# A fixed order for the end of the down projection: the last three row pieces transposed and squared in parts, their sums and scalings interleaved

## The chip, the cores and the metric

The kernel runs on one core of a Trainium2 chip. The metric is the device time of one execution in microseconds, the median of the runs.

## What is computed

One inference step of a one-layer decoder: a prompt of 1024 positions and 32 sample positions (1056 columns in all) pass through a mixer (windowed attention and retention) and a convolutional FFN. The change lies at the very end of the FFN, in its down projection and the norm behind it:

```python
h = jax.nn.gelu(a, approximate=True) * b
f = h @ w_down                           # 3072 -> 1024
x = x + rms_norm(f, g_post_ffn)          # rms_norm: f * rsqrt(mean(f*f) + EPS) * g
```

All of it is fp32. A product is made of three matmuls of operands split into a high and a low part (`mm3`).

## The kernel before

**Down projection.** `acc0` to `acc7` hold f transposed: each has 128 of the 1024 channels on its partitions and the 1056 positions along the free dimension. The product is computed by a Strassen-like scheme of seven products (`PORD`); S4 is the last. Within S4, `products(p, c, pt, js, ms)` does the k tiles of one third `pt` for one column half `j` and one channel tile (`c`, `e`), summed in a PSUM bank over `pt` 0 to 2. The last two tiles that come out complete are acc2 and then acc3, of the second half of the positions. acc3's last 264 columns are computed in two column pieces (`LASTP`): 136 and then 128 columns, each with 36 matmuls, and each added to acc3 by VectorE.

**Norm.** Rows (positions) are normalized in eleven pieces, `rws`. Pieces 0 to 4 come after S1; pieces 5, 6 and 7 (128, 128 and 16 rows) inside S4; pieces 8 (8 rows), 9 (128) and 10 (128) at the end: 8 and 9 lie in the 136 columns, 10 in the 128. `final` does one piece: eight transposes on TensorE turn columns of acc4 to acc7 (half 1) and of acc0 to acc3 (half 0) into two PSUM banks; ScalarE squares each bank into the tile `y` and sums the squares along the row; VectorE adds the two sums and makes the mean; GpSimd takes the power −1/2 (`rs`); VectorE multiplies each bank by `rs` and the gain into `y` (scaling); then x2 is added in halves (residual) and each half of `y` is written to HBM from SP's queue.

**Buffers.** `y` has three buffers (`tag="c_out", bufs=3`), so that piece 8 takes that of piece 5, 9 that of 6, 10 that of 7: the square of a piece overwrites what the write of the piece three back still reads. PSUM has eight banks in two rings of four: tag `m` for half 1 of the pieces, tag `t` for half 0; the products of the second position half use `t`.

```python
    def ps_8(j=0):
        return psum(p8, "mt"[j])
    for a, n, r in LASTP:
        for pt in range(3):
            products(S4, 1, pt, (1,), (1,), ws[pt], a, n)
        c12 = C(3, 0, 1, 1)[:, a:a + n]
        V.tensor_tensor(out=c12, in0=banks[1, 1, 1], in1=c12, op=add)
        norm(len(r), end=True)
```

**Order.** Each engine runs its instructions in a fixed order that a list scheduler makes at build time from a simulated timeline; `pin(ins)` keeps an instruction where the code has it in relation to other pinned ones of its engine. On the chip each engine waits at the first instruction whose inputs aren't there, and what is queued behind it on that engine waits too.

## Time and profile before

| | us |
|---|---|
| median of 3 runs | 1681.14 |
| the runs | 1680.82, 1681.14, 1684.15 |
| the profiled execution, its own time | 1684.12 |
| its span, from the first to the last instruction | 1682.3 |
| TensorE busy in the span | 1661.6 (99%) |

Busy time is a share of the span; a matmul's end is modelled, so a busy TensorE is not one at its peak. All durations below come from the one profiled execution, which took 2.98 us longer than the median, with 1.8 us of its time outside its span.

### The profile page before, as it was taken

The numbers are of one execution on the slowest core, as the hardware profiler recorded it, in microseconds if no ns is written. First come the engines' busy times: TensorE is split into PE (matmuls) and PEld (weight loads), VectorE is DVE, ScalarE is ACT, GpSimd is POOL, SyncE is SP. The second block draws the span as 40 slices with busy tenths as digits, with TensorE's granted clock in tenths as the row PEclk, the third lists the DMA queues.
The fourth block names the chain that finished last, engine by engine and source line by source line (L and its number), as shares of the span: only waits on it lengthen the run. The fifth ranks groups of instructions, "written<-read, shape, count | busy, mean of one in ns | idle before, by whom it ended". The sixth has DMA issues, their size and how long they took to land.

```text
span 1682.3 us, 31548 instructions
## 1 busy us (share of the span) xinstructions
PE 1661.6 (99%) x12257; PEld 1629.7 (97%) x12257; DVE 1181.2 (70%) x2305; ACT 794.4 (47%) x1727; POOL 341.1 (20%) x551
## 2 busy tenths in 40 slices
PE   8999999999999999999999999999999999999997
PEld 7999999999999999999888999999999999999997
DVE  7768554428586865658857888888888887455476
ACT  6576643223333332455433655555555556443343
POOL 4110110001212122320012412222221233111111
PEclk9999999999999999999999999999999999999999
DMA  7222234534242435377722145444444457866664
GB/s 198 64 74 80 74 97 123 180 106 145 96 152 95 151 102 173 109 247 239 234 94 87 45 156 161 148 155 149 146 146 146 149 162 246 257 183 199 192 184 149
DMA packets 253671, 247.87 MB, mean 147 GB/s; under 512 B 20192, under 2 KB 221568, under 8 KB 253505
## 3 DMA queue, kind: packets, MB, share of 16 engines
q1 hardware_dynamic: 224593, 145.10, 29.6%
q0 software_dynamic: 28928, 100.76, 17.4%
q8 instruction: 96, 1.57, 0.4%
q14 instruction: 54, 0.44, 0.1%
HBM read 171.27 MB, written 74.51 MB: 146 GB/s over the span
## 4 chain that ended last, share of the span: by engine, by line
PE 94%; DMA 2%; issue 2%; DVE 1%; POOL 0%; ACT 0%; SPq 0%; POOLq 0%; DVEq 0%; ACTq 0%
PE ps_mm L259 11%; PE ps_mm L261 11%; PE ps_mm L260 11%; PE ps_m L261 10%; PE ps_m L259 10%; PE ps_m L260 9%; PE ps_t L260 8%; PE ps_t L259 8%; PE ps_t L261 8%; PE ps_a L550 1%; PE ps_c L579 1%; DMA t<-z_d 1%; DMA a_in<-a_d 0%; PE ps_a L796 0%; PE ps_t L332 0%
## 5 line engine op out<-in xcount | busy, mean ns | idle before, releaser
L259 PE MATMUL ps_mm<-xh,w_hi 128*128 128x384 f32 (+1 forms) x888 | 291.8, 329 | 0.5 <-ACT w_hi L247 0.5
L261 PE MATMUL ps_mm<-xh,w_lo 128*128 128x384 f32 (+1 forms) x888 | 290.9, 328 | 0.0
L260 PE MATMUL ps_mm<-xl,w_hi 128*128 128x384 f32 (+1 forms) x888 | 289.5, 326 | 0.1
L227 DVE SCALAR_TENSOR_TENSOR w_lo<-w_raw,w_hi 128x1024 fp32r<-128x1024 f32 x115 | 140.5, 1222 | 115.6 <-ACT w_hi L232 62.8
L259 PEld LDWEIGHTS ps_mm<-xh,w_hi 128*128 128x128 f32 x888 | 168.1, 189 | 1.5 <-ACT w_hi L247 0.8
L260 PEld LDWEIGHTS ps_mm<-xl,w_hi 128*128 128x128 f32 x888 | 168.0, 189 | 1.2 <-issue 0.7
L261 PEld LDWEIGHTS ps_mm<-xh,w_lo 128*128 128x128 f32 x888 | 167.8, 189 | 0.6 <-issue 0.4
L259 PE MATMUL ps_t<-xh,w_hi 128*128 128x264 f32 (+2 forms) x524 | 148.9, 284 | 0.0
L260 PE MATMUL ps_t<-xl,w_hi 128*128 128x264 f32 (+2 forms) x524 | 148.7, 284 | 0.0
L261 PE MATMUL ps_t<-xh,w_lo 128*128 128x264 f32 (+2 forms) x524 | 148.0, 283 | 0.0
L261 PE MATMUL ps_m<-xh,w_lo 128*128 128x264 f32 x512 | 145.5, 285 | 1.3 <-DVE w_lo L227 1.3
L259 PE MATMUL ps_m<-xh,w_hi 128*128 128x264 f32 x512 | 145.7, 285 | 0.0
L260 PE MATMUL ps_m<-xl,w_hi 128*128 128x264 f32 x512 | 145.5, 284 | 0.0
L1233 DVE SCALAR_TENSOR_TENSOR c_out<-u_ext,fconst,c_out 128x1024 f32<-128x1024 f32 x96 | 121.9, 1279 | 2.2
L232 ACT CAST w_hi<-w_raw 128x1024 fp32r<-128x1024 f32 x62 | 65.2, 1052 | 105.6 <-PE ps_t L260 75.4
L261 PEld LDWEIGHTS ps_t<-xh,w_lo 128*128 128x128 f32 x524 | 98.7, 188 | 0.0
L260 PEld LDWEIGHTS ps_t<-xl,w_hi 128*128 128x128 f32 x524 | 98.6, 188 | 0.0
L259 PEld LDWEIGHTS ps_t<-xh,w_hi 128*128 128x128 f32 x524 | 98.6, 188 | 0.0
L261 PEld LDWEIGHTS ps_m<-xh,w_lo 128*128 128x128 f32 x512 | 96.3, 188 | 1.8 <-DVE w_lo L227 1.7
L259 PEld LDWEIGHTS ps_m<-xh,w_hi 128*128 128x128 f32 x512 | 96.2, 188 | 0.1
L260 PEld LDWEIGHTS ps_m<-xl,w_hi 128*128 128x128 f32 x512 | 96.2, 188 | 0.0
L286 POOL TENSOR_TENSOR rs<-ms,mhalf 128x1 f32<-128x1 f32 (+2 forms) x74 | 49.6, 671 | 226.4 <-DVE ms L284 225.9
(429 smaller groups left out, 5135.8 us busy)
## 6 DMA issues: line engine op xcount, KB each, us to landing
w_raw<-in_w_up SPq DMA_DIRECT2D x48, 512.0 KB, 4.7
w_raw<-in_w_in SPq DMA_DIRECT2D x42, 512.0 KB, 4.0
w_raw<-s_d SPq DMA_DIRECT2D x60, 256.0 KB, 3.5
t_d<-t POOLq DMA_DIRECT2D x24, 528.0 KB, 3.9
t<-t_d POOLq DMA_DIRECT2D x24, 528.0 KB, 5.0
t<-in_w_down SPq DMA_DIRECT2D x40, 256.0 KB, 4.7
s_d<-t POOLq DMA_DIRECT2D x20, 512.0 KB, 3.5
w_raw<-in_w_down SPq DMA_DIRECT2D x36, 256.0 KB, 5.0
```

The costliest lines, as they stand in the source:

```text
L227: pinned(V.scalar_tensor_tensor(out=out, in0=in0, scalar=1.0, in1=in1, op0=mult, op1=op))
L232: pinned(S.copy(out=hi, in_=src))
L259: TE.matmul(ps, wh, xh, start=start, stop=False, **kw)
L260: TE.matmul(ps, wh, xl, start=False, stop=False, **kw)
L261: TE.matmul(ps, wl, xh, start=False, stop=stop, **kw)
L286: G.tensor_tensor(out=rs[:r, :c], in0=ms[:r, :c], in1=mhalf[:r, :c], op=ALU.pow)
L550: TE.matmul(ps[:, jj, :], q, kS[s][v][:, kc], start=s == 0, stop=s == 1)
L579: TE.matmul(po[:, v], w, pr[:, s, 2 * v:2 * v + 2, :], start=i == 0 and s == 0, stop=i == len(ops) - 1 and s == 1)
L1233: V.scalar_tensor_tensor(out=c[:, NS:], in0=u[:, g, NU + t:NU + t + SEQ], scalar=sc[t], in1=c[:, NS:], op0=mult, op1=add)
```

## The change

`final` becomes a function that does the early part of a piece and returns three others: `rest` (the remaining sum and the power), `scale` and `residual`. For pieces 8, 9 and 10 the early part transposes and squares half 1 and, as a new and smaller square of 384 columns, what of half 0 is in acc0 to acc2; the last 128 columns, those of acc3, are transposed and squared in `rest`. The mean square is now built up in `ms` with one VectorE instruction a sum: `tensor_scalar` for the first, `scalar_tensor_tensor` for each further one (before: one addition, then one `tensor_scalar`). The early parts of all three pieces stand ahead of acc3's products. The products of the 136 columns get a bank of tag `m`, those of the 128 one of tag `t`, and the matmuls of the second, the late transposes, the sums, scalings and residuals are pinned. The order of the three pieces' scalings and residuals is written out by hand.

```diff
-    def mm3(ps, wh, wl, xh, xl, start, stop, **kw):
...
+    def mm3(ps, wh, wl, xh, xl, start, stop, order=None, **kw):
+        for w, x, a, b in ((wh, xh, start, False), (wh, xl, False, False), (wl, xh, False, stop)):
+            ins = TE.matmul(ps, w, x, start=a, stop=b, **kw)
+            if order is not None:
+                order(ins)
...
+    def transposes(ps, r0, n, ks, hf, last=False):
+        for k in ks:
+            ins = TE.transpose(ps[:n, k * P:(k + 1) * P], acc[4 * hf + k][:, r0:r0 + n], ident)
+            if last:
+                pin(ins)
+
+    def square(y, ps, n, hf, a, b, ss):
+        S.activation(y[:, 512 * hf + a:512 * hf + b], ps[:n, a:b], AF.Square, accum_out=ss)
...
+        def sums(i, hf, a, b):
+            if a == 0:
+                pss[hf] = ps_8(1 - hf)
+            transposes(pss[hf], r0, n, range(a, b), hf, a > 0)
+            square(y, pss[hf], n, hf, P * a, P * b, s2[:, i:i + 1])
+            if i == 0:
+                V.tensor_scalar(out=ms, in0=s2[:, 0:1], scalar1=1.0 / D, scalar2=EPS, op0=mult, op1=add)
+            else:
+                ins = V.scalar_tensor_tensor(out=ms, in0=s2[:, i:i + 1], scalar=1.0 / D, in1=ms,
+                                             op0=mult, op1=add)
+                if i == 2:
+                    pin(ins)
+
+        sums(0, 1, 0, 4)
+        sums(1, 0, 0, 3 if end else 4)
+
+        def rest():
+            if end:
+                sums(2, 0, 3, 4)
+            ins = G.tensor_tensor(out=r, in0=ms, in1=mhalf[:n, :1], op=ALU.pow)
+            if end:
+                pin(ins)
...
-    for a, n, r in LASTP:
-        for pt in range(3):
-            products(S4, 1, pt, (1,), (1,), ws[pt], a, n)
+    def last(i, pts):
+        a, n = LASTP[i][:2]
+        for pt in pts:
+            products(S4, 1, pt, (1,), (1,), ws[pt], a, n, i, pin if i else None)
+
+    def last_done(i):
+        a, n = LASTP[i][:2]
         c12 = C(3, 0, 1, 1)[:, a:a + n]
-        V.tensor_tensor(out=c12, in0=banks[1, 1, 1], in1=c12, op=add)
-        norm(len(r), end=True)
+        pin(V.tensor_tensor(out=c12, in0=banks[1, 1, 1], in1=c12, op=add))
+
+    k = rdone[0]
+    (rest0, sc0, res0), (rest1, sc1, res1), (rest2, sc2, res2) = (final(*rws[i], x2s[i], True)
+                                                                  for i in range(k, k + 3))
+    last(0, range(3))
+    last_done(0)
+    last(1, (0,))
+    rest0()
+    rest1()
+    last(1, (1, 2))
+    sc0(0)
+    res0(0)
+    last_done(1)
+    sc0(1)
+    rest2()
+    for f, x in ((sc1, 0), (res1, 0), (sc1, 1), (res0, 1), (sc2, 0), (res2, 0), (sc2, 1), (res1, 1),
+                 (res2, 1)):
+        f(x)
```

In the order rows below a number behind a tile's name tells buffers of one name apart. `y` and `s2` of piece 7 are 19455 and 19456 in both kernels.

TensorE, before, where acc2's products of 264 columns (into ps_t_19489) end and those of acc3's 136 columns begin:

```order
L261 MATMUL ps_t_19489<-xh_109,w_lo_19525 128x264
L259 MATMUL ps_t_19489<-xh_109,w_hi_19524 128x264
L260 MATMUL ps_t_19489<-xl_110,w_hi_19524 128x264
L261 MATMUL ps_t_19489<-xh_109,w_lo_19525 128x264
L259 MATMUL ps_t_19541<-xh_109,w_hi_19485 128x136
L260 MATMUL ps_t_19541<-xl_110,w_hi_19485 128x136
```

The same place of the changed kernel (its line 260 is the matmul of `mm3`, 1321 the transpose):

```order
L260 MATMUL ps_t_19489<-xl_110,w_hi_19524 128x264
L260 MATMUL ps_t_19489<-xh_109,w_lo_19525 128x264
L1321 MATMUL ps_t_19552<-ident_102,acc0_16787 8x128
L1321 MATMUL ps_t_19552<-ident_102,acc1_16788 8x128
L1321 MATMUL ps_t_19569<-ident_102,acc0_16787 128x128
L1321 MATMUL ps_t_19569<-ident_102,acc1_16788 128x128
L1321 MATMUL ps_m_19579<-ident_102,acc4_16783 128x128
L1321 MATMUL ps_m_19579<-ident_102,acc5_16784 128x128
L1321 MATMUL ps_m_19579<-ident_102,acc6_16785 128x128
L1321 MATMUL ps_m_19579<-ident_102,acc7_16786 128x128
L1321 MATMUL ps_t_19586<-ident_102,acc0_16787 128x128
L1321 MATMUL ps_t_19586<-ident_102,acc1_16788 128x128
```

Ten transposes of pieces 8, 9 and 10 (of acc0, acc1, and of acc4 to acc7 for piece 10) now stand between the two groups of products; before, the early ones of half 0 came after the 136-column products, and piece 10's after all products.

ScalarE, before, from the second square of piece 7 to the end (L1328; y_19579, y_19604 and y_19667 are pieces 8, 9 and 10):

```order
L1328 ACTIVATE y_19455,s2_19456<-ps_t_19463 16x512
L1328 ACTIVATE y_19579,s2_19580<-ps_m_19581 8x512
L1328 ACTIVATE y_19604,s2_19605<-ps_m_19606 128x512
L1328 ACTIVATE y_19579,s2_19580<-ps_t_19587 8x512
L1328 ACTIVATE y_19604,s2_19605<-ps_t_19612 128x512
L1328 ACTIVATE y_19667,s2_19668<-ps_m_19669 128x512
L1328 ACTIVATE y_19667,s2_19668<-ps_t_19675 128x512
```

And in the changed kernel, from the first square of piece 8 to the end (L1326; y_19541, y_19558 and y_19575 are pieces 8, 9 and 10):

```order
L1326 ACTIVATE y_19541,s2_19542<-ps_m_19545 8x512
L1326 ACTIVATE y_19558,s2_19559<-ps_m_19562 128x512
L1326 ACTIVATE y_19575,s2_19576<-ps_m_19579 128x512
L1326 ACTIVATE y_19541,s2_19542<-ps_t_19552 8x384
L1326 ACTIVATE y_19558,s2_19559<-ps_t_19569 128x384
L1326 ACTIVATE y_19575,s2_19576<-ps_t_19586 128x384
L1326 ACTIVATE y_19541,s2_19542<-ps_t_19552 8x128
L1326 ACTIVATE y_19558,s2_19559<-ps_t_19569 128x128
L1326 ACTIVATE y_19575,s2_19576<-ps_t_19586 128x128
```

The first square of piece 10 moved from behind all squares of pieces 8 and 9 to the third place, ahead of every square of half 0 of the three pieces, and half 0's squares are six of 384 and 128 columns in place of three of 512.

VectorE, before, from the last residual of piece 7 through the completion of acc3's last 128 columns (the second row of L1423):

```order
L1337 TENSOR_TENSOR y_19455<-y_19455,x2_19205 16x512
L1423 TENSOR_TENSOR acc3_16790<-ps_t_19541,acc3_16790 128x136
L1331 TENSOR_TENSOR s2_19580<-s2_19580 8x1
L284 TENSOR_SCALAR ms_19594<-s2_19580 8x1
L1331 TENSOR_TENSOR s2_19605<-s2_19605 128x1
L284 TENSOR_SCALAR ms_19619<-s2_19605 128x1
L1335 SCALAR_TENSOR_TENSOR y_19579<-ps_t_19587,rs_19596,g_pf_18227 8x512
L1335 SCALAR_TENSOR_TENSOR y_19579<-ps_m_19581,rs_19596,g_pf_18227 8x512
L1423 TENSOR_TENSOR acc3_16790<-ps_t_19629,acc3_16790 128x128
```

The same stretch of the changed kernel, from just behind piece 7's last residual (L1342 and L1344 make the mean squares, L1466 completes acc3, L1361 scales):

```order
L1342 TENSOR_SCALAR ms_19560<-s2_19559 128x1
L1342 TENSOR_SCALAR ms_19577<-s2_19576 128x1
L1344 SCALAR_TENSOR_TENSOR ms_19543<-s2_19542,ms_19543 8x1
L1344 SCALAR_TENSOR_TENSOR ms_19560<-s2_19559,ms_19560 128x1
L1344 SCALAR_TENSOR_TENSOR ms_19577<-s2_19576,ms_19577 128x1
L1466 TENSOR_TENSOR acc3_16790<-ps_m_19592,acc3_16790 128x136
L1344 SCALAR_TENSOR_TENSOR ms_19543<-s2_19542,ms_19543 8x1
L1344 SCALAR_TENSOR_TENSOR ms_19560<-s2_19559,ms_19560 128x1
L1361 SCALAR_TENSOR_TENSOR y_19541<-ps_t_19552,rs_19544,g_pf_18227 8x512
L1466 TENSOR_TENSOR acc3_16790<-ps_t_19630,acc3_16790 128x128
```

The early sums of all three pieces, piece 10's (ms_19577) last, now stand ahead of the addition that completes acc3's 136 columns; before, that addition stood first.

VectorE, before, from there to its end:

```order
L1335 SCALAR_TENSOR_TENSOR y_19604<-ps_t_19612,rs_19621,g_pf_18227 128x512
L1335 SCALAR_TENSOR_TENSOR y_19604<-ps_m_19606,rs_19621,g_pf_18227 128x512
L1337 TENSOR_TENSOR y_19579<-y_19579,x2_19329 8x512
L1331 TENSOR_TENSOR s2_19668<-s2_19668 128x1
L1337 TENSOR_TENSOR y_19604<-y_19604,x2_19453 128x512
L284 TENSOR_SCALAR ms_19682<-s2_19668 128x1
L1335 SCALAR_TENSOR_TENSOR y_19667<-ps_t_19675,rs_19684,g_pf_18227 128x512
L1335 SCALAR_TENSOR_TENSOR y_19667<-ps_m_19669,rs_19684,g_pf_18227 128x512
L1337 TENSOR_TENSOR y_19667<-y_19667,x2_19480 128x512
```

And in the changed kernel:

```order
L1466 TENSOR_TENSOR acc3_16790<-ps_t_19630,acc3_16790 128x128
L1361 SCALAR_TENSOR_TENSOR y_19541<-ps_m_19545,rs_19544,g_pf_18227 8x512
L1344 SCALAR_TENSOR_TENSOR ms_19577<-s2_19576,ms_19577 128x1
L1361 SCALAR_TENSOR_TENSOR y_19558<-ps_t_19569,rs_19561,g_pf_18227 128x512
L1361 SCALAR_TENSOR_TENSOR y_19558<-ps_m_19562,rs_19561,g_pf_18227 128x512
L1368 TENSOR_TENSOR y_19541<-y_19541,x2_19329 8x512
L1361 SCALAR_TENSOR_TENSOR y_19575<-ps_t_19586,rs_19578,g_pf_18227 128x512
L1361 SCALAR_TENSOR_TENSOR y_19575<-ps_m_19579,rs_19578,g_pf_18227 128x512
L1368 TENSOR_TENSOR y_19558<-y_19558,x2_19453 128x512
L1368 TENSOR_TENSOR y_19575<-y_19575,x2_19480 128x512
```

Before, piece 10's scalings stood behind both residuals of pieces 8 and 9; now only piece 8's residual stands ahead of them, and the residuals of pieces 9 and 10 come last together.

## Rows read from the trace of the kernel before

**Rows 1.** The page: its first line, the busy time of the engines, and the chain that ended last by engine.

```profile
span 1682.3 us, 31548 instructions
...
PE 1661.6 (99%) x12257; PEld 1629.7 (97%) x12257; DVE 1181.2 (70%) x2305; ACT 794.4 (47%) x1727; POOL 341.1 (20%) x551
...
PE 94%; DMA 2%; issue 2%; DVE 1%; POOL 0%; ACT 0%; SPq 0%; POOLq 0%; DVEq 0%; ACTq 0%
```

**Rows 2.** The instructions in order of time on TensorE, where the last products of the program end. Columns: start in us, duration in us, engine, line, operation, tile written and tiles read, shape, count, and the idle time before it with what ended it. L259 to L261 are the three matmuls of `mm3`, L1327 the transposes of `final`.

```profile
1661.97 0.28 PE L261 MATMUL ps_t<-xh,w_lo 128*128 128x264 f32 x1
1662.09 0.23 PE L259 MATMUL ps_t<-xh,w_hi 128*128 128x136 f32 x1
...
1665.95 0.28 PE L261 MATMUL ps_t<-xh,w_lo 128*128 128x136 f32 x1
1666.06 0.82 PE L1327 MATMUL ps_t<-ident,acc 128*8 128x128 f32 x6
1666.64 0.31 PE L259 MATMUL ps_t<-xh,w_hi 128*128 128x128 f32 x1
...
1668.57 0.38 PE L1327 MATMUL ps_t<-ident,acc 128*8 128x128 f32 x2
...
1670.75 0.28 PE L261 MATMUL ps_t<-xh,w_lo 128*128 128x128 f32 x1
1670.86 0.62 PE L1327 MATMUL ps_m<-ident,acc 128*128 128x128 f32 x4
...
1672.28 0.33 PE L1327 MATMUL ps_t<-ident,acc 128*128 128x128 f32 x1 [0.46 <-DVE acc L1423]
```

**Rows 3.** The chain that ended last in order of time, one of its pieces: start in us, us that it holds the chain, engine, tile, line, count.

```profile
1657.03 0.87 PE ps_m L1327 x8
```

**Rows 4.** The instructions in order of time on VectorE at the same place, columns as in the second group. L1335 scales, L1337 adds the residual, L1423 completes acc3, L1331 and L284 make the mean square.

```profile
1662.45 0.73 DVE L1335 SCALAR_TENSOR_TENSOR y<-ps_m,rs,g_pf 16x512 f32<-16x512 f32 x1
...
1671.30 0.73 DVE L1335 SCALAR_TENSOR_TENSOR y<-ps_m,rs,g_pf 8x512 f32<-8x512 f32 x1
1671.96 0.27 DVE L1423 TENSOR_TENSOR acc<-ps_t,acc 128x128 f32<-128x128 f32 x1
1672.15 0.73 DVE L1335 SCALAR_TENSOR_TENSOR y<-ps_t,rs,g_pf 128x512 f32<-128x512 f32 x1
...
1673.47 1.30 DVE L1337 TENSOR_TENSOR y<-y,x 8x512 f32<-8x512 f32 x1
1674.70 0.14 DVE L1331 TENSOR_TENSOR s<-s 128x1 f32<-128x1 f32 x1
1674.77 0.67 DVE L1337 TENSOR_TENSOR y<-y,x 128x512 f32<-128x512 f32 x1
1675.37 0.13 DVE L284 TENSOR_SCALAR ms<-s 128x1 f32<-128x1 f32 x1
1676.23 0.75 DVE L1335 SCALAR_TENSOR_TENSOR y<-ps_t,rs,g_pf 128x512 f32<-128x512 f32 x1 [0.73 <-POOL rs L286]
...
1677.67 1.20 DVE L1337 TENSOR_TENSOR y<-y,x 128x512 f32<-128x512 f32 x1
```

**Rows 5.** The same view of GpSimd (L286 the power −1/2 on one column, L1337 the residual of a first half).

```profile
1672.96 1.26 POOL L1337 TENSOR_TENSOR y<-y,x 128x512 f32<-128x512 f32 x1 [0.25 <-DVE y L1335]
1675.65 0.55 POOL L286 TENSOR_TENSOR rs<-ms,mhalf 128x1 f32<-128x1 f32 x1 [1.42 <-DVE ms L284]
1677.06 1.26 POOL L1337 TENSOR_TENSOR y<-y,x 128x512 f32<-128x512 f32 x1 [0.86 <-DVE y L1335]
```

**Rows 6.** The same view of ScalarE (L232 casts weights, L1328 squares with a sum, whose read-out is an instruction of its own).

```profile
1655.20 1.06 ACT L232 CAST w_hi<-w_raw 128x1024 fp32r<-128x1024 f32 x1 [1.84 <-PE ps_t L260]
...
1656.73 0.59 ACT L1328 ACTIVATE y<-ps_t 128x512 f32<-128x512 f32 x1
...
1657.30 0.57 ACT L1328 ACTIVATE y<-ps_m 16x512 f32<-16x512 f32 x1
...
1664.11 0.60 ACT L1328 ACTIVATE y<-ps_m 128x512 f32<-128x512 f32 x1 [5.00 <-DMA out_y_prompt<-y]
...
1672.65 0.60 ACT L1328 ACTIVATE y<-ps_t 128x512 f32<-128x512 f32 x1 [0.38 <-PE ps_t L1327]
1673.14 0.20 ACT L1328 ACTIVATION_READ_ACCUMULATOR y<-ps_t 128x1 f32 x1
```

**Rows 7.** The writes of y to HBM (L1339, on SP's queue), one stretch of time after another: name and count, duration of the issue in ns (min/median/max), first and last start in us; and the us from issue to landing. First the second write of piece 7, then three writes of pieces 8 and 9, then the last write of the program.

```profile
L1339 SPq DMA_DIRECT2D out_y_prompt<-y x1: 331/331/331, 1664.8 to 1664.8; - x1
...
DMA to landing us min/median/max: 2.5/2.5/2.5
...
L1339 SPq DMA_DIRECT2D out_y_prompt<-y x3: 283/355/382, 1674.8 to 1675.6; - x3
...
DMA to landing us min/median/max: 2.1/2.2/2.3
...
L1339 SPq DMA_DIRECT2D out_y_prompt<-y x1: 332/332/332, 1678.9 to 1678.9; - x1
```

**Rows 8.** ScalarE and then VectorE in order of time some 40 us earlier, where S4's weights are split into w_hi and w_lo.

```profile
1630.12 1.05 ACT L232 CAST w_hi<-w_raw 128x1024 fp32r<-128x1024 f32 x1 [1.28 <-PE ps_m L260]
1633.05 1.06 ACT L232 CAST w_hi<-w_raw 128x1024 fp32r<-128x1024 f32 x1 [1.87 <-PE ps_m L260]
...
1631.41 1.22 DVE L227 SCALAR_TENSOR_TENSOR w_lo<-w_raw,w_hi 128x1024 fp32r<-128x1024 f32 x1
```

More of the change, by code (lines that the diff above doesn't have):

```diff
@@ L256, in wcols @@
         return weights(k, n, [(lambda r: r, src)], **kw)
-    def mm3(ps, wh, wl, xh, xl, start, stop, **kw):
-        TE.matmul(ps, wh, xh, start=start, stop=False, **kw)
-        TE.matmul(ps, wh, xl, start=False, stop=False, **kw)
-        TE.matmul(ps, wl, xh, start=False, stop=stop, **kw)
+    def mm3(ps, wh, wl, xh, xl, start, stop, order=None, **kw):
[3 more added lines that the diff above has]
+                order(ins)
     def sample_cols(t):
@@ L1321, in final @@
         y = fp.tile([P, D], F32, name="y", tag="c_out", bufs=3)[:n]
-        s2 = sml.tile([P, 2], F32, name="s2")[:n]
+        s2 = sml.tile([P, 4], F32, name="s2")[:n]
         pss = {}
-        for hf in (1, 0):
-            ps = ps_8(1 - hf)
-            for k in range(4):
-                TE.transpose(ps[:n, k * P:(k + 1) * P], acc[4 * hf + k][:, r0:r0 + n], ident)
-            S.activation(y[:, 512 * hf:512 * hf + 512], ps[:n], AF.Square,
-                         accum_out=s2[:, hf:hf + 1])
-            pss[hf] = ps
@@ L1331, in final @@
-        V.tensor_tensor(out=s2[:, 0:1], in0=s2[:, 0:1], in1=s2[:, 1:2], op=add)
-        r = rsqrt_mean(s2[:, 0:1], D, n, 1)
-        for hf in range(2):
-            nn = slice(512 * hf, 512 * hf + 512)
-            V.scalar_tensor_tensor(out=y[:, nn], in0=pss[hf][:n], scalar=r, in1=g_pf[:n, nn],
-                                   op0=mult, op1=mult)
-            (G if end and hf == 0 else V).tensor_tensor(out=y[:, nn], in0=y[:, nn], in1=x2[:, nn],
-                                                        op=add)
+        ms, r = (sml.tile([P, 16], F32, name=q)[:n, :1] for q in ("ms", "rs"))
@@ new lines, in final, with scale @@
+        sums(0, 1, 0, 4)
[6 more added lines that the diff above has]
+                pin(ins)
+        def scale(hf):
+            nn = slice(512 * hf, 512 * hf + 512)
+            ins = V.scalar_tensor_tensor(out=y[:, nn], in0=pss[hf][:n], scalar=r, in1=g_pf[:n, nn],
+                                         op0=mult, op1=mult)
+            if end:
+                pin(ins)
@@ L1339, in final, with residual @@
+        def residual(hf):
+            nn = slice(512 * hf, 512 * hf + 512)
+            ins = (G if end and hf == 0 else V).tensor_tensor(out=y[:, nn], in0=y[:, nn], in1=x2[:, nn],
+                                                              op=add)
+            if end:
+                pin(ins)
             ld.dma_start(out=dst[:, nn], in_=y[:, nn])
+        return rest, scale, residual
     rws = ROWS_A22 + ROWS_S4 + [r for d in LASTP for r in d[2]]
@@ L1343, in trunk, with norm @@
     rdone = [0]
-    def norm(n, end=False):
+    def norm(n):
         for _ in range(n):
@@ L1349, in norm @@
             rdone[0] += 1
-            final(*rws[i], x2s[i], end)
+            rest, scale, residual = final(*rws[i], x2s[i])
+            rest()
+            for hf in range(2):
+                scale(hf)
+                residual(hf)
             if i + 3 < len(rws):
@@ L1373, in trunk, with products @@
     banks = {}
-    def products(p, c, pt, js, ms=(0, 1), w=None, a=0, n=HW):
+    def products(p, c, pt, js, ms=(0, 1), w=None, a=0, n=HW, bank=None, order=None):
         hi, lo = down_weights(p, c, pt) if w is None else w
@@ L1382, in products @@
                 if first and pt == 0:
-                    banks[key] = ps_8(j)[:, :n]
+                    banks[key] = ps_8(j if bank is None else bank)[:, :n]
                 ps = banks[key]
@@ L1387, in products @@
                     mm3(ps, hi[:, 4 * e + k], lo[:, 4 * e + k], hh[:, k, a:a + n], hl[:, k, a:a + n],
-                        first and pt == 0 and k == 0, pt == 2 and k == 3, skip_group_check=not first)
+                        first and pt == 0 and k == 0, pt == 2 and k == 3, order, skip_group_check=not first)
                 if pt == 2 and n == HW:
```

## The prediction

> **What bounds the kernel now.** The page first: TensorE is busy 99% of a span of 1682.3 us and holds 94% of the chain that ended last, so for nearly all of the time only what delays TensorE counts [rows 1]. The change lies in the last 20 us, which I read engine by engine in order of time. TensorE starts acc3's 136-column products at 1662.09, the 128-column ones at 1666.64, and begins its last matmul at 1670.75; it ends 0.28 later, at 1671.03 [rows 2]. Behind that TensorE bounds nothing any more. VectorE does: it is still scaling piece 8 when the last products end, so that the addition to acc3 starts at 1671.96, 0.93 late; piece 10's last square ends at 1673.34, but its sum starts only at 1674.70, behind piece 8's residual, which took 1.30; its scalings start at 1676.23, and the last residual ends at 1678.87 [rows 4, 6]. So the span has two parts to cost: TensorE up to 1671.03, and a tail of 7.84 us from there to the last residual, with the write to HBM behind it.
>
> The upstream stages keep their order except for one swap of two matmuls and a few VectorE and SP instructions. Of these the largest move is a weight part w_lo that started at 1631.41 and now stands behind two scalings, about 1.8 later. The three weight buffers turn over every 2.93 us (casts at 1630.12 and 1633.05, each when a buffer comes free), so the part is wanted two turns, 5.9 us, after 1630.1, at 1636.0; it ended at 1632.6 and would end at 1634.4 [rows 8]. That hides it: cost 0. Without that cover it would cost what it is late.
>
> **The change, part by part.**
>
> *More transposes ahead of the last product.* Between the 264-column products and the end of the last ones TensorE did 6 + 2 transposes [rows 2]; now it does 10 + 3 + 2 = 15 (the order rows show the ten). A transpose holds the chain 0.87 / 8 = 0.109 [rows 3]; seven more are **+0.76**, in line on TensorE and hidden by nothing. They are the same transposes that came after the last product, so this is a move, and the tail below is shorter for it.
>
> *The bank of the 136-column products.* It now is of ring `m`, the one that piece 7's second scaling frees. That ended at 1663.18 [rows 4], and one more VectorE sum (0.14; the one-column operations took 0.13 and 0.14 [rows 4]) now stands ahead. TensorE comes there at 1662.09 + 10 × 0.109 = 1663.18, the bank is free at 1663.32 and a little: **+0.2**. Bounds 0 (the sum falls into VectorE's wait for the power) and 0.35.
>
> *A new wait for a write to HBM.* Piece 10's first square writes the `y` buffer that piece 7's writes read. Before, it came at the end and found them long landed; the same wait is in the trace for piece 9, where ScalarE sat idle 5.00 us until a write had landed [rows 6]. Piece 7's second write was issued at 1664.8 and took 2.5 to land [rows 7]: 1667.3, and with the 0.14 from above 1667.4. ScalarE starts about 0.1 later, at 1667.55. All six squares of half 0 stand behind it on ScalarE, and on VectorE piece 10's two sums stand ahead of the addition that completes acc3's 136 columns, for which the next transposes on TensorE wait. Squares follow each other at 0.57 (1656.73 to 1657.30); a column costs (1.06 − 0.60) / 512 = 0.9 ns by the cast and the square of rows 6, so 384 columns are 0.115 less, 0.455; from start to read-out end a square of 512 is 0.69, one of 384 is 0.575 [rows 6]. The third 384-column square ends at 1667.55 + 0.57 + 2 × 0.455 + 0.575 = 1669.6, piece 10's sum starts with it, acc3's addition at 1669.75, and TensorE resumes 0.32 after that (1671.96 to 1672.28 [rows 2, 4]) at 1670.1. TensorE gets there from 1663.38 by 24 matmuls of (1666.06 − 1662.09) / 36 = 0.110, 3 transposes, 12 more matmuls at 0.110 and 12 of the 128-column kind at 0.111, at 1669.0 [rows 2, 3]. The stall is **+1.1**. Bounds: 0 if the write lands by 1666.3, and 1.6 if the squares cost the full 512 price and the write lands 0.1 later than there.
>
> By the Trainium skill, "DMA: Bandwidth & Descriptors", section "Anatomy of one DMA", a transfer costs about 2.0 us and bytes at 436 GB/s; for 32 KB that would be an estimate of 2.1 in place of the 2.5 traced, the stall 0.7 and the sum 0.4 smaller. The trace's own durations, 2.1 to 2.6 for the late writes, decide here.
>
> *The tail, from the end T of the last product.* VectorE is free, so the addition starts at T + 0.05 (before + 0.93). From it to the last square 0.69 as before (1671.96 to 1672.65). That square has 128 columns: 0.69 − 384 × 0.9 ns = 0.345, and its sum follows at once: T + 1.1 (before T + 3.67). But the sum no longer opens piece 10's scalings. VectorE first has piece 9's two scalings (starts 0.67 apart, T + 1.2 to T + 2.55), then piece 8's residual. GpSimd starts piece 9's residual 0.83 after the first of these scalings (1676.23 to 1677.06), holds 1.26, and the trace shows what VectorE's residual then does: it took 1.30 and 1.20 where it overlapped GpSimd's (each ended 0.55 after GpSimd's end at 1674.22 and 1678.32), and 0.67 beside an idle GpSimd [rows 4, 5]. So piece 8's residual ends at T + 2.05 + 1.26 + 0.55 = T + 3.85. Piece 10's scalings follow to T + 5.15; its power was ready long before. GpSimd's residual of piece 10 runs from T + 4.65 to T + 5.9, piece 9's residual on VectorE ends at T + 6.45, piece 10's at T + 7.05. Against 7.84 that is **−0.8**. Bounds: −1.6 (piece 8's residual meets no GpSimd work, and one sum more is hidden) and +0.3 (128 columns squared at the 512 price, and each start 0.1 later).
>
> *The last writes.* SP issues in order: piece 9's second half at T + 6.5, piece 10's two halves behind it. Three issues took from 1674.8 to 1675.6, 0.4 apart [rows 7], so the last starts at T + 7.3; the last of before started at 1678.9, T + 7.87. That is 0.2 less of a gain than the residuals' 0.8, and three 256 KB writes in 0.8 us, where there were two in about 0.6, cost some 0.15 more to land: **+0.35**, between 0 and 0.7.
>
> *Sum.* 0.76 + 0.2 + 1.1 − 0.8 + 0.35 = **+1.6**. The other additions (three squares, three sums) lie in these steps or beside TensorE's products. On the profiled execution, 1684.12 with 1682.3 of span, this is a span of 1683.9 and 1685.7; on the median of the runs, 1681.14, it is **1682.75**, 0.1% more. I take the difference for both, since the 2.98 between them is outside the steps. What a measurement of this kernel can tell from no change is about 0.2%, 3.4 us: its three runs alone lie 3.3 apart. The lower bounds add up to 0.76 − 1.6 = −0.8, the upper ones to 0.76 + 0.35 + 1.6 + 0.3 + 0.7 = +3.7: the likeliest case's own range is 1680.3 to 1684.8.
>
> **The rivals.**
>
> *The write lands in time or the squares are early enough, no stall.* Then the sum is +0.5: **1681.65**. For it speaks that 1.1 is the difference of two long estimates (1670.1 and 1669.0); against it, that the landing would have to come 1.1 earlier than traced, which the traced 2.1 to 2.6 do not reach. Chance 0.2.
>
> *Faster: VectorE and GpSimd don't get in each other's way.* If piece 10's chain were alone behind T, with no stall ahead, it would need 1.2 to its sum, 0.8 for the power (1675.65 + 0.58, [rows 4, 5]), 1.35 for the scalings and 0.67 for one residual: about T + 4.9 with gaps, 2.9 less than before; with the transposes' 0.76 that is −2.2, **1678.95**. It decides from the point where both other residuals on VectorE are over before piece 10's scalings. Against it are two rows of 1.30 and 1.20 and the order itself, in which two residuals of pieces 8 and 9 still precede piece 10's. Chance 0.05. Even this end is within 0.2%.
>
> The Trainium skill, "SBUF — State Buffer", section "Who interferes with whom", says that a VectorE instruction with two SBUF inputs and a GpSimd instruction that reads SBUF exclude each other for their whole length; by that rule the two overlaps of my tail stand, and the trace's 1.30 against 0.67 agrees.
>
> *Slower by more than 0.2%: the landing is later still.* Each microsecond that piece 7's write lands later is one on TensorE, for everything to the end stands behind it. From +1.6 it takes 1.8 more, a landing 4.3 after the issue, to pass 3.4; **1684.6** and up. For it speaks that a load of x2 is issued right behind that write; against it, that no late write took over 2.6 [rows 7]. Chance 0.06. Beside it stands the runs' own scatter: one of three lay 3 us above the others, and a median that falls there would be 1685.7 with my sum. Chance 0.1.
>
> **How the numbers follow.** My case has 0.59, no stall 0.2, faster 0.05, slower by the landing 0.06, the scatter 0.1. The prediction is the first one's 1682.75. The range leaves out the faster rival's lower half and what lies beyond the scatter's: 1679.6 to 1685.4. All but the last two cases lie within 3.4 us of 1681.14, a little of the first two beyond their bounds: same 0.83; slower by over 0.2% 0.13 (most of the last two); faster by over 0.2% 0.04, for a tail cheaper than any row here bounds.
>
> **What would show it.** In the changed kernel's trace: ScalarE idle for some 2.5 us before piece 10's first square, put down to a write of y; TensorE idle about 1.1 us before the transposes of acc3 for pieces 8 and 9, put down to acc3's addition or to ScalarE; the last matmul ending near 1673.1; acc3's last addition within 0.1 of it; two residuals on VectorE at 1.2 to 1.3; the last residual near 1680.2, and a span of about 1683.9. I am wrong in mechanism if TensorE doesn't stall there, and wrong in the tail if the last residual comes less than 6.2 or more than 8.1 after the last matmul.

## The result and the profile after

The changed kernel took 1686.4 us in the median of 20 runs, the one before 1682.78 beside it on the same chip, a ratio of 1.0019 (95% interval 1.0013 to 1.0025): 3.2 us slower by the ratio, where I had forecast +1.6. Three later series of the same program gave 1.0017, 1.0020 and 1.0018 (below). The profiled execution, at 1684.47 with 1682.7 of span, is only 0.35 above the profiled one of before, so this pair of traces shows neither the full loss nor, at first sight, where it is.

The page of the changed kernel, its first line and the chain that ended last by engine:

```profile
span 1682.7 us, 31570 instructions
...
PE 92%; DMA 2%; issue 2%; DVE 1%; ACT 1%; POOL 1%; SPq 0%; DVEq 0%; ACTq 0%; POOLq 0%
```

The chain now has 92% on TensorE and not 94% [rows 1]. The spans alone mislead: from about 850 us on, matmul after matmul starts 1.5 us earlier than before, a lead that arises with the first loads and in waits hundreds of us ahead of the change and has nothing to do with it. So I count from the last place that the change leaves alone, the eight transposes with which the first halves of pieces 8 and 9 begin, ahead of the last 264-column products. Before, and then after, on TensorE:

```profile
1656.87 1.04 PE L1327 MATMUL ps_m<-ident,acc 128*8 128x128 f32 x8
```

```profile
1655.40 1.04 PE L1321 MATMUL ps_m<-ident,acc 128*8 128x128 f32 x8
...
1661.71 0.33 PE L260 MATMUL ps_m<-xh,w_hi 128*128 128x136 f32 x1
...
1667.29 0.27 PE L260 MATMUL ps_t<-xh,w_lo 128*128 128x128 f32 x1
1668.38 0.38 PE L1321 MATMUL ps_t<-ident,acc 128*8 128x128 f32 x2 [0.82 <-DVE acc L1466]
...
1671.12 0.27 PE L260 MATMUL ps_t<-xh,w_lo 128*128 128x128 f32 x1
1671.87 0.30 PE L1321 MATMUL ps_t<-ident,acc 128*128 128x128 f32 x1 [0.47 <-DVE acc L1466]
```

From there to the end of the span it was 1682.3 − 1656.87 = 25.4 us before and is 1682.7 − 1655.40 = 27.3 now: **+1.85**, in place of the predicted 1.6. TensorE comes to the 136-column products at 1661.71 behind the ten transposes and waits for nothing there; before the two transposes of acc3 it stands idle for 0.82, put down to the addition that completes acc3's 136 columns; and the last product ends at 1671.39, which I again call T. ScalarE, VectorE and GpSimd in the same stretch:

```profile
1665.77 0.60 ACT L1326 ACTIVATE y<-ps_m 128x512 f32<-128x512 f32 x1 [2.47 <-DMA out_y_prompt<-y]
...
1667.28 0.46 ACT L1326 ACTIVATE y<-ps_t 128x384 f32<-128x384 f32 x1
```

```profile
1667.95 0.29 DVE L1466 TENSOR_TENSOR acc<-ps_m,acc 128x136 f32<-128x136 f32 x1
...
1671.43 0.29 DVE L1466 TENSOR_TENSOR acc<-ps_t,acc 128x128 f32<-128x128 f32 x1 [0.75 <-PE ps_t L260]
...
1672.60 0.16 DVE L1344 SCALAR_TENSOR_TENSOR ms<-s,ms 128x1 f32<-128x1 f32 x1 [0.24 <-ACT y L1326]
...
1674.04 1.37 DVE L1368 TENSOR_TENSOR y<-y,x 8x512 f32<-8x512 f32 x1
...
1676.66 1.95 DVE L1368 TENSOR_TENSOR y<-y,x 128x512 f32<-128x512 f32 x2
```

```profile
1673.60 1.27 POOL L1368 TENSOR_TENSOR y<-y,x 128x512 f32<-128x512 f32 x1
1676.21 1.26 POOL L1368 TENSOR_TENSOR y<-y,x 128x512 f32<-128x512 f32 x1 [1.34 <-DVE y L1361]
```

The wait for the write is there as forecast: ScalarE stood idle for 2.47 us before piece 10's first square, until piece 7's write of y had landed; half 0's squares of 384 columns and the sums follow, and the addition to acc3's 136 columns comes at 1667.95, 0.8 too late for TensorE. The writes of y on SP's queue, piece 7's second one with its us from issue to landing, and then the last three:

```profile
L1372 SPq DMA_DIRECT2D out_y_prompt<-y x1: 331/331/331, 1663.2 to 1663.2; - x1
...
DMA to landing us min/median/max: 2.4/2.4/2.4
```

```profile
L1372 SPq DMA_DIRECT2D out_y_prompt<-y x3: 356/378/398, 1678.0 to 1679.0; - x3
```

Issued at 1663.2 and 2.4 on the way, piece 7's write let ScalarE go at 1665.77. So this one trace comes within 0.25 us of the sum, in part because its misses offset each other (below), and the runs say twice as much. That is what the experiments had to explain.

### The profile page after: what moved, and what is told of

It is laid out like the page before. It is cut to its first block, busy times and chain, and to the rows that moved or that the text cites. A ratio compares the mean times of both kernels' runs of the same rounds, so it can differ in the third digit from the quotient of the medians.

```text
span 1682.7 us, 31570 instructions
## 1 busy us (share of the span) xinstructions
PE 1660.1 (99%) x12257; PEld 1627.9 (97%) x12257; DVE 1181.9 (70%) x2308; ACT 793.8 (47%) x1733; POOL 339.8 (20%) x551
## 4 chain that ended last, share of the span: by engine, by line
PE 92%; DMA 2%; issue 2%; DVE 1%; ACT 1%; POOL 1%; SPq 0%; DVEq 0%; ACTq 0%; POOLq 0%
PE ps_mm L260 33%; PE ps_m L260 28%; PE ps_t L260 23%; PE ps_b L260 1%; PE ps_a L551 1%; PE ps_c L580 1%; PE ps_a L260 1%; DMA t<-z_d 1%; DMA s<-in_state_ret 0%; PE ps_t L333 0%; PE ps_c L767 0%; PE ps_a L797 0%; PE ps_a L821 0%; PE ps_b L567 0%; PE ps_a L333 0%
## 5 line engine op out<-in xcount | busy, mean ns | idle before, releaser
L260 PE MATMUL ps_m<-xh,w_lo 128*128 128x264 f32 (+1 forms) x524 | 149.1, 285 | 0.7 <-DVE w_lo L227 0.6
L260 PE MATMUL ps_m<-xh,w_hi 128*128 128x264 f32 (+1 forms) x524 | 149.0, 285 | 0.0
L260 PE MATMUL ps_m<-xl,w_hi 128*128 128x264 f32 (+1 forms) x524 | 148.8, 284 | 0.0
L260 PE MATMUL ps_t<-xh,w_hi 128*128 128x264 f32 (+1 forms) x512 | 145.6, 284 | 0.0
L260 PE MATMUL ps_t<-xl,w_hi 128*128 128x264 f32 (+1 forms) x512 | 145.3, 284 | 0.0
L260 PE MATMUL ps_t<-xh,w_lo 128*128 128x264 f32 (+1 forms) x512 | 144.7, 283 | 0.0
L232 ACT CAST w_hi<-w_raw 128x1024 fp32r<-128x1024 f32 x62 | 65.2, 1051 | 104.4 <-PE ps_t L260 73.8
L260 PE MATMUL ps_m<-ex,w 128*128 128x264 f32 x792 | 107.4, 284 | 0.0
L260 PE MATMUL ps_t<-xh,w 128*128 128x264 f32 x528 | 107.0, 283 | 0.0
L260 PE MATMUL ps_m<-xh,w 128*128 128x264 f32 x528 | 107.0, 284 | 0.0
L260 PE MATMUL ps_t<-ex,w 128*128 128x264 f32 x792 | 107.0, 283 | 0.0
```

What stands on the lines that cost most here:

```text
L232: pinned(S.copy(out=hi, in_=src))
L260: ins = TE.matmul(ps, w, x, start=a, stop=b, **kw)
```

## The experiments

All were timed against the kernel before; "from the eight transposes" is the distance from their start to the end of the span in each trace (25.45 before, 27.30 after).

**Both kernels again.** What one trace can't tell may be scatter, so both ran once more beside the first experiments.

> The kernel before, unchanged, against itself. All theories: a ratio of 1.0000 within 0.05%; its interval says how far two equal programs can lie apart. A second trace of the end is wanted: from the eight transposes of pieces 7 and 8 at 1656.87 to the end of the span it took 25.4 us in the first one; the tail theory expects 25.4 within 0.3 again. Upstream it may differ by 1 to 3 us (the first loads, and the load that the state products wait for near 645 us).

> The changed kernel, unchanged. Tail theory (all of the change is in the last 27 us, where the two traces differ by 1.9 us): ratio 1.0011, 27.3 us from the same transposes to the end. Rival (part of the difference lies elsewhere, in the stages ahead or in a TensorE clock that falls at the new stalls in executions other than the profiled one): ratio 1.0019 to 1.0021 again, with a lower mean clock than the kernel before, or a trace whose matmuls fall behind before 1650 us.

Before against itself: 1.0002 (0.9993 to 1.0010), from the eight transposes (they are of pieces 8 and 9, not of 7 and 8 as the expectation has it) 25.44. After: 1.0017 (1.0007 to 1.0027), from the eight transposes **29.1**, 1.8 more than in its first trace. ScalarE's wait for the write and TensorE in this trace, and the granted clock (the number behind POOL's) by the microsecond:

```profile
1667.27 0.60 ACT L1326 ACTIVATE y<-ps_m 128x512 f32<-128x512 f32 x1 [2.85 <-DMA out_y_prompt<-y]
```

```profile
1669.88 0.38 PE L1321 MATMUL ps_t<-ident,acc 128*8 128x128 f32 x2 [1.24 <-DVE acc L1466]
...
1673.51 0.41 PE L260 MATMUL ps_t<-xl,w_hi 128*128 128x128 f32 x1
1673.72 0.41 PE L260 MATMUL ps_t<-xh,w_lo 128*128 128x128 f32 x1
1674.61 0.45 PE L1321 MATMUL ps_t<-ident,acc 128*128 128x128 f32 x1 [0.48 <-DVE acc L1466]
```

```profile
1670.00:1671.00 1.00, 1.00 (x11) 1.00 (x11) 0.31 (x2) 0.61 (x4) 0.13 (x1) 1.00 0.00 0
1671.00:1672.00 1.00, 1.00 (x8) 1.00 (x8) 0.55 (x1) 0.00 (x0) 0.93 (x2) 0.70 0.00 0
1672.00:1673.00 1.00, 1.00 (x6) 1.00 (x7) 0.19 (x1) 0.00 (x0) 0.68 (x1) 0.50 0.00 0
```

The write, issued 7.8 after the eight transposes as in the first trace, took 2.9 to land and not 2.4, and TensorE's idle time is 1.24 and not 0.82, 0.4 of the difference. Most of the rest is not waiting: the clock, full at the resumption, is 0.70 in the microsecond from 1671 and 0.50 from 1672, the 1.2 GHz level; from there on the last 11 matmuls start 0.21 apart where those ahead stand 0.11 apart, and from the two transposes to the last one it is 4.73 us (1669.88 to 1674.61) in place of 3.49 (1668.38 to 1671.87), 1.24 more. In the first trace the clock was still full in the microsecond of the last transpose:

```profile
1671.00:1672.00 1.00, 0.53 (x5) 0.39 (x4) 0.57 (x2) 0.00 (x0) 1.00 (x1) 1.00 0.00 0
```

From here there were two theories. The first: piece 7's late write makes TensorE wait, and behind the wait its clock falls in a part of the executions, so that the loss is wait plus clock. The rival: the wait and the longer order cost all of it, and the clock only happens to fall.

**A buffer of its own for piece 10.** Piece 10's `y` no longer shares the three buffers that the writes hold; nothing else changes.

```
-        y = fp.tile([P, D], F32, name="y", tag="c_out", bufs=3)[:n]
+        if end and r0 == rws[-1][0]:
+            y = tr.tile([P, 4, HW], F32, name="t0").rearrange("p k c -> p (k c)")[:n, :D]
+        else:
+            y = fp.tile([P, D], F32, name="y", tag="c_out", bufs=3)[:n]
```

> The changed kernel with one edit: piece 10's y lies in a buffer of its own, so that its first square waits for no write to HBM; the order of every engine stays. Theory (the wait for piece 7's write costs TensorE 0.8 us at the transposes of acc3): ScalarE's 2.5 us of idle and TensorE's 0.82 are gone, 26.4 to 26.6 us from the transposes at the fork to the end, time 0.8 us (0.05%) below the changed kernel. Rival (the stall lies beside other work and costs nothing): TensorE's stall goes, but the last write comes no earlier. Rival (the stall lets TensorE's clock fall in some executions): 2 us or more below the changed kernel and a higher mean clock.

Ratio 1.0001 (0.9992 to 1.0010), from the eight transposes 26.3. (One of its twelve runs took 7878.14 us; the ratio leaves it out, and nothing here shows its cause.) ScalarE and TensorE at the place:

```profile
1664.35 0.60 ACT L1326 ACTIVATE y<-ps_m 128x512 f32<-128x512 f32 x1 [4.95 <-DMA out_y_prompt<-y]
...
1664.94 0.59 ACT L1326 ACTIVATE t<-ps_m 128x512 f32<-128x512 f32 x1
```

```profile
1669.17 0.38 PE L1321 MATMUL ps_t<-ident,acc 128*8 128x128 f32 x2
```

Piece 10's square (into `t`) follows piece 9's at once, and TensorE runs into the two transposes without idle time. Against after beside it the runs are 3.1 us faster by the means (95% interval ±1.4), where the wait alone was to cost 0.8, and their mean clock is 0.9964 and not 0.9952. So the buffer that waits for the write is the root of most of the loss: without it the new order costs nothing that these runs tell from zero, though the trace still has 0.9 more than before from the eight transposes on.

**One sum out of the way.** The prediction had VectorE's queue carry the delay to TensorE: piece 10's sum stands ahead of acc3's addition. Here that sum stands behind it.

```
+    late = []
...
-            if i == 0:
+            if end and i == 1 and r0 == rws[-1][0]:
+                late.append(lambda: pin(V.scalar_tensor_tensor(out=ms, in0=s2[:, 1:2], scalar=1.0 / D, in1=ms,
+                                                               op0=mult, op1=add)))
+            elif i == 0:
...
     last_done(0)
+    late.pop()()
```

> The changed kernel with one edit: piece 10's second sum stands behind the addition that completes acc3's 136 columns on VectorE, in place of ahead of it; ScalarE still waits for the write. Theory (the stall reaches TensorE by VectorE's queue): the addition starts about 0.5 us earlier, when piece 9's sum is done, and TensorE's stall falls from 0.8 to 0.3 or 0.4; 0.4 us less in all. Rival (the stall comes by ScalarE's squares, whose banks the transposes write): TensorE's stall stays above 0.7.

ScalarE from piece 10's first square, VectorE's addition and TensorE at the two transposes:

```profile
1665.99 0.60 ACT L1326 ACTIVATE y<-ps_m 128x512 f32<-128x512 f32 x1 [2.94 <-DMA out_y_prompt<-y]
...
1667.50 0.46 ACT L1326 ACTIVATE y<-ps_t 128x384 f32<-128x384 f32 x1
```

```profile
1667.70 0.29 DVE L1471 TENSOR_TENSOR acc<-ps_m,acc 128x136 f32<-128x136 f32 x1
```

```profile
1668.14 0.38 PE L1321 MATMUL ps_t<-ident,acc 128*8 128x128 f32 x2 [0.77 <-ACT y L1326]
```

The wait, 0.77 and put down to ScalarE, looks like the rival's. But the write took 2.9 to land in this execution, as in the second trace of after, where TensorE stood idle for 1.24. Counted from piece 10's 384-column square, the addition comes 0.20 later (1667.50 to 1667.70), where it came 0.67 later in the first trace of after (1667.28 to 1667.95), and TensorE resumes 0.64 later and not 1.10. From the addition to TensorE it is 0.44 here and 0.43 there: as far as these distances tell, it is still the addition that lets TensorE go, and the name of ScalarE is that of an event close beside it (the square that ends then is piece 10's, in a bank that these two transposes don't write). So the queue did carry the delay, and the edit took some 0.46 from the wait, about as expected. The ratio, 1.0012 (1.0003 to 1.0020), is 2.0 us below after beside it by the means (±1.4). That is more than 0.46; a clock that falls less often would suit it, which one trace, with the full clock, does not show.

**Two thirds of the last products ahead of the transposes.** Twelve more matmuls give the squares 1.3 us.

```
-    last(1, (0,))
+    last(1, (0, 1))
     rest0()
     rest1()
-    last(1, (1, 2))
+    last(1, (2,))
```

> The changed kernel with one edit: the transposes of acc3 for pieces 8 and 9 stand behind two thirds of the last products in place of one, so that TensorE has 12 more matmuls (1.3 us) to do while piece 10's first square waits for the write. Theory (a stall of TensorE before its last products, and in a part of the executions half the clock after it, make the change slow): no stall, full clock to the last product, time as with the buffer of its own, ratio 0.9998 to 1.0008. Rival (the wait of ScalarE itself costs, wherever TensorE is): no better than 1.0012.

The wait before the two transposes is gone, and the clock stays full, but the trace is shorter by 0.1 only (27.2 from the eight transposes), because acc3's last addition now stands behind a scaling of piece 8, and the last transpose waits 0.98 for it where it waited 0.47 (VectorE, then TensorE):

```profile
1670.41 0.74 DVE L1361 SCALAR_TENSOR_TENSOR y<-ps_t,rs,g_pf 8x512 f32<-8x512 f32 x1 [0.46 <-POOL rs L1355]
1671.08 0.27 DVE L1466 TENSOR_TENSOR acc<-ps_t,acc 128x128 f32<-128x128 f32 x1
```

```profile
1668.84 0.38 PE L1321 MATMUL ps_t<-ident,acc 128*8 128x128 f32 x2
...
1671.49 0.30 PE L1321 MATMUL ps_t<-ident,acc 128*128 128x128 f32 x1 [0.98 <-DVE acc L1466]
```

The ratio, 1.0009 (1.0000 to 1.0018), falls between the two expectations. The wait was moved; against after beside it the runs gained 1.8 us by the means (±1.5), which the first theory puts down to the clock, but the interval doesn't settle it.

**A longer wait.** The transposes ahead of all the last products: the wait grows and 36 matmuls stand behind it.

```
-    last(1, (0,))
     rest0()
     rest1()
-    last(1, (1, 2))
+    last(1, (0, 1, 2))
```

> The changed kernel with one edit the other way: the same two transposes stand ahead of all of the last products, so that TensorE gets there 1.3 us earlier and waits 1.3 us longer (2.1 us or more). Clock theory: the clock falls to half behind the stall in nearly all executions, and 36 matmuls of 0.11 us then take up to 0.22: ratio 1.0030 to 1.0050, mean clock 0.994 or lower. Rival (only the stall itself costs): 1.3 us above the changed kernel, ratio 1.0023 to 1.0028, mean clock as in the changed kernel.

TensorE from the two transposes to the last one, and two of the microseconds between:

```profile
1669.82 0.59 PE L1321 MATMUL ps_t<-ident,acc 128*8 128x128 f32 x2 [2.38 <-DVE acc L1466]
...
1678.45 0.45 PE L1321 MATMUL ps_t<-ident,acc 128*128 128x128 f32 x1 [0.47 <-DVE acc L1466]
```

```profile
1669.00:1670.00 1.00, 0.18 (x2) 0.21 (x3) 0.37 (x2) 0.27 (x2) 0.00 (x0) 0.59 0.00 0
...
1677.00:1678.00 1.00, 0.98 (x5) 0.79 (x4) 0.00 (x0) 0.00 (x0) 0.00 (x0) 0.50 0.00 0
```

1.0038 (1.0025 to 1.0050), where a wait alone would have given up to 1.0028, which the interval doesn't exclude; the trace tells more. After an idle time of 2.38 the clock is 0.59 in the very microsecond of the resumption and 0.50 to the end of the products; 8.63 us pass from the first transposes to the last.

**The idle time filled.** The cleanest separation: the transposes come as late, but TensorE does matmuls meanwhile. Three products are added a second time ahead of the transposes (those columns of y come out too large).

```
     last(1, (0,))
+    hh, hl = XS[(6 * PORD.index(S4) + 1) % 8]
+    for q in range(3):
+        mm3(banks[1, 1, 1], ws[0][0][:, 4 + q], ws[0][1][:, 4 + q], hh[:, q, LASTP[1][0]:LASTP[1][0] + LASTP[1][1]],
+            hl[:, q, LASTP[1][0]:LASTP[1][0] + LASTP[1][1]], False, False, pin)
     rest0()
```

> The changed kernel with nine 128-column matmuls more on TensorE right ahead of the transposes that wait (three products of pt 0 are added a second time, so those columns of y come out too large; nothing else is left out or moved). They take 9 x 0.111 = 1.0 us, about the 0.8 to 1.2 for which TensorE stood idle there, so everything behind that point begins when it began before, or up to 0.2 us later; only TensorE no longer stands idle ahead of its last 24 matmuls. Theory (half of the loss is the clock that falls behind the stall): trace: under 0.3 us idle ahead of those transposes, the granted clock 1.00 until the last product, the 24 matmuls and what lies between them in 3.5 us and not 4.7; ratio to the kernel before 1.0003 to 1.0013, mean clock of the runs 0.996 or more. Rival (the wait itself and what is late with it cost all of the 0.19%, the clock is a bystander): the same time as the changed kernel or 0.2 us more, ratio 1.0016 to 1.0024.

> The changed kernel itself, once more, beside the kernel with the nine matmuls on the same chip. Both theories: ratio 1.0015 to 1.0022, 0.8 to 1.2 us idle ahead of the transposes that wait. By the theory of the clock a trace with the shorter wait shows the full clock up to the last product, one with the longer wait half of it; the mean clock of the runs is 0.995 to 0.9957.

TensorE with the nine matmuls, at the two transposes and the last one, and the windows where the products run; then the same of after beside it:

```profile
1667.88 0.38 PE L1321 MATMUL ps_t<-ident,acc 128*8 128x128 f32 x2
...
1671.36 0.30 PE L1321 MATMUL ps_t<-ident,acc 128*128 128x128 f32 x1 [0.47 <-DVE acc L1466]
```

```profile
1670.00:1671.00 1.00, 0.89 (x8) 0.74 (x7) 0.25 (x2) 0.00 (x0) 0.69 (x1) 1.00 0.00 0
```

```profile
1668.10 0.38 PE L1321 MATMUL ps_t<-ident,acc 128*8 128x128 f32 x2 [1.20 <-DVE acc L1466]
...
1672.45 0.45 PE L1321 MATMUL ps_t<-ident,acc 128*128 128x128 f32 x1 [0.47 <-DVE acc L1466]
```

```profile
1671.00:1672.00 1.00, 0.97 (x5) 0.78 (x4) 0.00 (x0) 0.00 (x0) 0.79 (x1) 0.50 0.00 0
```

With the nine matmuls the ratio is 1.0009 (1.0000 to 1.0018), without them on the same chip 1.0018 (1.0007 to 1.0029). The kernel that does more work takes less time: against the 30 later runs of after, whose mean is 1686.06, its 11 average 1684.03, 2.0 less, with a 95% interval of about ±1.0 (against the 10 beside it on the same chip 2.1, ±1.4). From the eight transposes its trace has 27.5, and 3.48 from the two transposes to the last, as at full clock; after's trace beside it has 28.7 and 4.35, at the lower level. The rival, at 1.0016 or more, is at the interval's upper end, and it has no reason for a gain. I take the first theory as shown: filling the wait, without ending it, gives back some 2 of the 3.5 us by which after lies above before by the means. How the loss divides between wait and clock is known no better than that ±1.0.

**After once more,** beside the second group of experiments:

> The changed kernel again, beside the other three on the same chip: 1.0017 to 1.0020. Clock theory: a third trace shows one of the two ends seen so far, either full clock to the last product and about 25.6 us from the fork to the end, or half clock from the stall and about 27.5.

1.0020 (1.0010 to 1.0031). Its trace had the shorter wait, 0.77, and the full clock; from the eight transposes 27.25. So of four traces of the same program two show the full clock (waits of 0.82 and 0.77; 27.3 from the eight transposes) and two the lower one (1.24 and 1.20; 29.1 and 28.7). The write was issued 7.8 to 7.9 after the eight transposes in all four and took 2.4 to land in the first two, 2.9 and 2.8 in the others. The runs' mean clocks over the whole span point the same way: 0.9950 to 0.9956 in the three later series of after, 0.9968 in those of before and 0.9966 with the filled idle time. But they can't place the loss. The trace with piece 10's own buffer has 0.995 with all its products at the full clock; and the spread is in before as well: of the 30 runs of after the eight with 0.994 average 1688.1 and the three with 0.997 1683.1, of the 82 runs of before beside them the four with 0.995 average 1685.1 and the 25 with 0.998 1680.7.

**A version that keeps what is good of the order.** With the own buffer, piece 8's and piece 9's second residuals are put behind piece 10's scalings, and piece 10's first residual goes to VectorE, so that no VectorE residual meets one of GpSimd's. The reordering (the buffer's edit, and the one that moves piece 10's residual, are left out here):

```
+    sc0(1)
     last_done(1)
-    sc0(1)
+    sc1(0)
     rest2()
-    for f, x in ((sc1, 0), (res1, 0), (sc1, 1), (res0, 1), (sc2, 0), (res2, 0), (sc2, 1), (res1, 1),
-                 (res2, 1)):
+    for f, x in ((res1, 0), (sc1, 1), (sc2, 0), (sc2, 1), (res2, 0), (res2, 1), (res0, 1), (res1, 1)):
```

> The changed kernel with piece 10's y in a buffer of its own and another order of the tail: piece 8's scalings ahead of acc3's last addition, piece 9's around piece 10's sum, piece 10's scalings right behind, and then the four residuals left on VectorE one after another, with nothing on GpSimd beside them. Theory (the two meetings with GpSimd cost 0.6 us each, and piece 8's residual stands ahead of piece 10's scalings): the last residual 5.9 us after the last product in place of 7.2, ratio 0.9990 to 0.9998. Rival (what bounds the tail is the last writes): the residuals end earlier, the span does not, ratio 1.0001.

VectorE from acc3's last addition to the end:

```profile
1672.99 0.29 DVE L1469 TENSOR_TENSOR acc<-ps_t,acc 128x128 f32<-128x128 f32 x1
...
1676.38 1.28 DVE L1371 TENSOR_TENSOR t<-t,x 128x512 f32<-128x512 f32 x2
1677.58 1.27 DVE L1371 TENSOR_TENSOR y<-y,x 8x512 f32<-8x512 f32 x2
```

Four residuals in a row at 0.64 each; the last ends 5.9 after acc3's last addition began, where it was 7.2 after (1671.43 to 1678.61) and 6.9 before [rows 4]. From the eight transposes 24.2, the shortest of all traces and 1.2 less than before. The runs: 0.9998 (0.9990 to 1.0007), which can't be told from before and doesn't decide between the theory and the rival (the trace, shorter by 1.2, is for the theory); against after beside it, 1.0020, it is 3.9 us faster by the means (±1.4).

## Why the prediction was half right

Slower was forecast, by a mechanism that the traces show step by step, and within 0.2%, where most of the chance lay; 0.19% is at the edge of that. The time itself, 1686.4, lies 3.6 above the 1682.75 and outside the range: 1.6 of it because before, over 20 runs, has 1682.8 and not the 1681.14 of its three runs (the scatter, to which the prediction gave 0.1), and 2 because the change cost twice what I summed. That the first trace came so near the sum, +1.85 against +1.6, is partly luck: TensorE's part was 0.2 smaller, the tail and the last writes 0.2 and 0.3 larger.

*Transposes ahead and the bank.* To T it is 1671.39 − 1655.40 = 15.99 now and 14.16 before: +1.83 against +2.06. To the 136-column products it is 6.31 after the eight transposes, before 1662.09 − 1656.87 = 5.22: 1.09 for ten transposes, as costed, and nothing for the bank, where I had 0.2. Two and three transposes follow where there were eight, −0.33; the wait holds up the next start by 0.98 (1667.29 + 0.11 to 1668.38; the idle time of 0.82 counts from the modelled end).

*The wait for the write: the step that failed.* The path was right to the instruction: 2.47 of idle ScalarE, its squares, the sums on VectorE, the addition, the transposes. In the first trace it held TensorE up by 0.98, predicted 1.1. What is wrong is what I took a wait on TensorE to cost: its own length, in every execution. The idle time varied from 0.77 to 1.24 and ScalarE's from 2.46 to 2.91, with the landing of the write, and in a part of the executions the clock fell behind it, so that the last 11 (second trace) or 7 (the trace beside the filled one) of the 24 matmuls took 0.21 and not 0.11. The term, sized +1.1, measured 1.0 in that trace and 0.4 + 1.2 more in the second; by the runs it is about 3, since without it (piece 10's own buffer) after lies 3.1 ± 1.4 us lower. A hint of that price stood in the trace of before, where TensorE had waited for a state 1000 us earlier:

```profile
649.25 0.58 PE L796 MATMUL ps_a<-s0s,h 128*128 128x256 f32 x1 [2.84 <-ACT s0s L232]
```

```profile
644.00:648.00 4.00, 2.41 (x21) 2.20 (x19) 0.90 (x3) 0.00 (x0) 0.73 (x1) 1.00 0.95 300
...
652.00:656.00 4.00, 4.00 (x23) 4.00 (x23) 1.60 (x5) 0.37 (x1) 1.50 (x2) 0.57 0.41 144
```

There too the clock was full up to the wait and low behind it. I had read that place as one that the change doesn't touch, not as a price list. Yet it prices a wait of 2.84 us only; behind one of 0.70 in the same trace the clock stayed full (1.00 from 788 to 794 us):

```profile
789.87 0.39 PE L261 MATMUL ps_m<-xh,w_lo 128*128 128x264 f32 x1 [0.70 <-DVE w_lo L227]
```

So the rows of before left open what follows a wait of 1.1, and the term needed a bound for that. The Trainium skill, "TensorE: Matmul & The Clock Gate", Part 1: The HAM clock gate, says of a kernel's start that how many matmuls run slow differs from run to run of one kernel. Two traces of after in four show the like behind a wait at its end.

*Bound by the wrong rows.* The upper bound of 1.6 for that wait came from the squares' price and a landing 0.1 later, and knew no price for what follows a wait. The rival "the landing is later still" had the right sign and place and half of the lever: the landing was 0.4 to 0.5 later in two traces of four, above the 2.6 that the prediction took for the longest, but it passes on to TensorE one for one only until the clock falls. The 2.0 us and bytes of the Trainium skill, "DMA: Bandwidth & Descriptors", section "Anatomy of one DMA", which the prediction set beside the traced 2.5, is there a fit for DMAs issued from GpSimd. This write, issued from SP's queue, took 2.4 to 2.9.

*The tail.* 7.22 from T to the last residual's end, predicted 7.05, before 7.84: −0.62 and not −0.8. Piece 10's sum came at T + 1.2 (predicted 1.1), piece 8's residual took 1.37 beside GpSimd's 1.27 and ended at T + 4.0 (3.85). The last pair again meets one of GpSimd's, 1.95 for two; alone a residual took 0.64. The Trainium skill's rule in "SBUF — State Buffer", section "Who interferes with whom", which I had cited, holds in both.

*The last writes.* From the last residual to the end 4.09 against 3.45, +0.64 in place of +0.35: three issues from 1678.0 to 1679.0 are 0.5 apart, not 0.4, and from the last of them to the end it is 3.7, before 3.4 (1678.9 to 1682.3). The 0.15 that the prediction had for the latter was a guess for which no row stood.

Upstream, the swapped matmuls and the later w_lo cost nothing that the traces show, as forecast.

## What to carry to other kernels

When work that squares, scales or evicts is pulled ahead of the last matmuls, look up which buffer it writes and when the last reader of that buffer, a write to HBM perhaps, is through: here three shared buffers turned a move of 0.8 us into a loss of over 3, and a fourth one took most of it away. Price a wait on a busy TensorE not by its length alone but with the matmuls behind it at the lower clock. And where that can go either way from one execution to the next, two profiles aren't enough to account for a difference of 0.2%: line them up at the last common place, and look at the granted clock of that stretch, since a run's mean clock does not say where it was low. Where a wait is put down to an engine, check it against the distance to the other candidates: in the run with the sum out of the way the name alone would have led to the wrong verdict.

## What was not expected of the hardware

A TensorE that had been busy at the full clock and then stood idle for 1.24 and 1.20 us did the first 13 and 17 of its next 24 matmuls at the full clock and the last 11 and 7 at the 1.2 GHz level; after 0.82 and 0.77 at the same place all 24 had the full clock. With the sum out of the way the write landed as late as in the first two (2.9), TensorE stood idle for 0.77 only, and the clock stayed full: it went with the idle time, not with the landing. These are four traces of one program and one of another; what decides it, and how often each comes, stays open (the runs' distance of 3.5 us from before by the means, beside 1.85 in a trace at full clock and 3.7 and 3.2 in the two without, would suit the lower clock in more than half of them). Executions differ in TensorE's clock elsewhere too: near 650 us, in the 20 us from 640, it is 0.83 in one trace of before and 0.91 in the other.
